# Second norm as a stream of its own and the first FFN unit's sums in PSUM, in a two-path transformer block on one core

## The chip, the cores and the metric

One core of a Trainium2 chip runs the whole program. The metric is the device time of one execution in microseconds (us), the median of several runs. Before the change it is 1468.44 us.

## What is computed

One layer is applied to two groups of rows: 1024 rows of a sample and 128 rows of a prompt, each 1024 wide, all in fp32. A mixer with three head groups (Fourier, mLSTM, S5) is followed by one output projection and a gated residual, then by a modulated norm and a SwiGLU network. Cut to what matters here:

```python
def block(x, mods, p, init, grid):
    sh1, sc1, g1, sh2, sc2, g2 = mods
    xn = rmsnorm(x, p["norm1_w"]) * (1 + sc1) + sh1
    mix, final = mixer(xn, p, init, grid)
    x = x + g1 * mix
    xn = rmsnorm(x, p["norm2_w"]) * (1 + sc2) + sh2
    ff = (jax.nn.silu(xn @ p["w_gate"]) * (xn @ p["w_up"])) @ p["w_down"]
    x = x + g2 * ff
    return x, final
```

The change lies between `x + g1 * mix` and the first of the products with `w_gate` and `w_up`.

## The kernel before, in words

**How the order of the work is made.** The kernel is written as a set of Python generators ("streams"), each with a priority, that yield single instructions. `Weaver.run` (L200) keeps modelled clocks of the engines and at each turn emits the head of the stream that could start first; at equal times the lower priority number goes first. What it emits is the fixed order of each engine's queue, and on the chip each engine takes its queue in that order. A stream waits with `has("name")` for a milestone of another one, `take`/`push`/`used` hand tiles from stream to stream, and `bank` takes one of the eight PSUM banks. An operation given the engine `VP` goes to VectorE or to GpSimd, whichever the model takes to end first. Because every instruction is recorded by one helper, all rows of the profile have the line L146, and tiles' names tell the work apart.

**fp32 products.** `split` (L264) writes a tile as a high part (ScalarE, a cast) and a low part (VectorE, source minus high part). `mm3` makes one product of three matmuls: high × low, low × high, high × high. A product over 512 features is four blocks of 128, that is 12 matmuls of 512 columns.

**The output projection** (`out_project`, L1454) goes in two column halves; in the second, each of the nine row chunks c (0 to 7 the sample, 8 the prompt) has 24 matmuls into one bank. `evac_x1` (L1538) takes a bank: `gt` = bank × gate, `xr` += `gt`, a square with a sum on ScalarE, and `ss`, the sum over both column halves. `xr` are the tiles of x1, five buffers; `x1_feed` (L1529) loads them, and chunks 5 to 8 can only be loaded when earlier buffers come free (`used("x1")`).

**The second norm.** `scaled` (L1549) makes 1/rms of some chunks (`ms`, `y` by pow on GpSimd, `t`, `t`, `t`, `r`) and multiplies the tiles. `affined` (L1554) transposes a 128-column block of four chunks into a bank (four matmuls with `ident`) and writes it through ScalarE with the modulation's scale and shift, to `xt`. `norm_h0` (L1562) does this for chunks 0 to 3, eight blocks k, and splits each block at once into Y11 and Y21 (`y200f`/`y201f` and `y210f`/`y211f` in the profile). `norm_h1` (L1576) starts behind it, with chunks 4 to 7: blocks 0 to 3 give b12, of which Y11's difference T1 is made, blocks 4 to 7 give b22, split into Y22 (`y220f`/`y221f`); then T2, T3 and T4 follow, sums and differences of these blocks for a seven-product scheme. `norm_p` (L1636) does the prompt's chunk 8, eight single transposes (`xtp`, split into `yp00t`/`yp01t`).

**The FFN units.** There are eleven units of 256 hidden columns, each with a gate half and an up half. `weights1` (L1659) splits the raw weights `fraw` into `r10t`/`r11t` (`r0`, upper half of the features), `r20t`/`r21t` (`r1`) and, from unit 1 on, sums `sd` into `sh`/`sl`. The first unit (`first_unit`, L1745) runs plain products: per half and for each of its two 128-column parts d, Y11 with r0, Y21 with r1, T1 with r0 and Y22 with r1; each product has a bank of its own and VectorE adds it in SBUF (`pu`, or `xr` in the up half). T1's result is 12 minus 11, so its sum starts from Y11's. The prompt's products (256 columns) come between. The later units (`gate_or_up`, L1805) run the seven-product scheme. `prompt_store` (L1721) turns the prompt's hidden rows `hp` of the unit before with two transposes and stores them; it is called in `gate_or_up` (L1855) behind the first product of each gate half.

Of the kernel before, what the change touches and what calls it, by code (L numbers as in the profile page):

```python
# [111 lines left out]
class Weaver:  # L112
# [47 lines left out]
    def has(self, *names):  # L160
        return lambda: all(n in self.done for n in names)
# [59 lines left out]
def tile_trunk(ctx, tc, I, O, dbg=None):  # L221
# [61 lines left out]
    def used(name):  # L283
        wv.fed[name][1] += 1
# [1264 lines left out]
    def scaled(cs):  # L1549
        r = yield from rstd_of(ss2[:, cs[0]:cs[-1] + 1], len(cs), D, f"r1{len(cs)}")  # L1550
        for i, c in enumerate(cs):
            yield ts(V, x1[c], x1[c], r[:, i:i + 1], ALU.mult)

    def affined(cs, k, t):  # L1554
        ps, = yield from bank([128, len(cs), 128], keep=1)
        yield [T.transpose(ps[:, i], x1[c][:, k * 128:(k + 1) * 128], ident) for i, c in enumerate(cs)]
        yield has(f"affine1{k // 4}")
        ab, st = AB[2 + k // 4], int(cs[0] == 8)
        yield act(t, ps, AF.Identity, scale=ab[:, k % 4, 0, st:st + 1], bias=ab[:, k % 4, 1, st:st + 1])
        give(ps)  # L1560

    def norm_h0():  # L1562
        yield has(*[f"x1_{c}" for c in range(4)])
        yield from scaled(range(4))
        for k in range(8):
            if k % 4 == 0:
                yield has(f"ob{k // 4}")
                Y["12"[k // 4] + "1"] = [unit("f", k // 4, n, "y2", (4, 512)) for n in range(2)]
            t = xw.tile([128, 512], F32, name="xt", bufs=4)
            yield from affined(range(4), k, t)  # L1570
            hi, lo = Y["12"[k // 4] + "1"]
            yield from split(t, hi[:, k % 4], lo[:, k % 4], V)
        for _ in range(4):
            used("x1")

    def norm_h1():  # L1576
        yield has(*[f"x1_{c}" for c in range(4, 8)], "norm_h0")
        yield from scaled(range(4, 8))
        KS = range(4)
        part = {q: [[u[:, k] for u in Y[q]] for k in KS] for q in ("11", "21")}  # L1580

        def f(q, k):
            return [u.bitcast(F32) for u in part[q][k]]

        def unit_of(i, name):
            yield has(f"wo{i}")
            return wo_unit(i, name).rearrange("p (k t) -> p k t", k=4)

        def new(q, *at):
            us = []  # L1590
            for n, i in enumerate(at):
                us.append((yield from unit_of(i, f"{q}{n}")))
            Y[q] = us
            part[q] = [[u[:, k] for u in us] for k in KS]
        b12 = []
        for k in KS:
            b12.append(xw.tile([128, 512], F32, name="xt", bufs=4))
            yield from affined(range(4, 8), k, b12[k])
            d = xw.tile([128, 512], F32, name="xd", bufs=2)
# [6 lines left out]
        b22 = (yield from unit_of(2, "b22")).bitcast(F32)  # L1606
        for k in KS:
            yield from affined(range(4, 8), k + 4, b22[:, k])
# [4 lines left out]
        for _ in range(4):  # L1613
            used("x1")
        done.update(("22", "x1used"))
# [10 lines left out]
        done.update(("T2", "T3"))  # L1626
        yield from new("T4", 7, 2)
        for k in KS:
            d, e = (xw.tile([128, 512], F32, name=n, bufs=b) for n, b in (("xd", 2), ("xt", 4)))
            yield tt(VP, d, f("21", k)[0], f("T2", k)[0], ALU.subtract)  # L1630
            yield tt(VP, e, f("21", k)[1], f("T2", k)[1], ALU.subtract)
            yield tt(VP, d, d, e, ALU.add)
            yield from split(d, *part["T4"][k], VP)
        done.add("T4")

    def norm_p():  # L1636
# [105 lines left out]
                yield from gate_or_up(i, up, sg, pg)  # L1742


    def first_unit():  # L1745
        gate, val, pg = {}, {}, []
        for up in range(2):
            r0 = yield from take("r0")
            ab = []
            for d in range(2):  # L1750
                ps, = yield from bank([128, 512])
                yield from prod(ps, [t[:, :, d] for t in r0], "11")
                if d == 0:
                    yield has("x1used" if up else "fpu")
                if up:
                    t = xw.tile([128, D], F32, name="xr", bufs=5)
                    ab.append((t[:, 0:512], t[:, 512:1024]))
                else:
                    ab.append([L5["fpu"].tile([128, 512], F32, name="pu", bufs=4) for _ in range(2)])
                yield act(ab[d][1], ps, AF.Copy)  # L1760
                give(ps)

            def finish(q, t):
                if not up:
                    yield act(t, t, AF.Silu)
                    gate[q] = t
                else:
                    yield tt(VP, t, t, gate[q], ALU.mult)
                    val[q] = t

            def rest(r, q, last):
                for d in range(2):
                    ps, = yield from bank([128, 512])
                    yield from prod(ps, [t[:, :, d] for t in r], q)
                    o = ab[d][0 if q == "21" else 1]
                    yield tt(V, o, ab[d][1], ps, ALU.add)
                    give(ps)
                    if last:
                        yield from finish(2 * d + (q != "21"), o)
            r1 = yield from take("r1")  # L1780
            yield from rest(r1, "21", True)
            yield has("T1")
            yield from rest(r0, "T1", False)
            bp, = yield from bank([128, 2, 128], keep=1)
            yield from prompt(bp, 0, r0)
            used("r0")
            yield has("22")
            yield from rest(r1, "22", True)
            yield from prompt(bp, 1, r1)
            used("r1")  # L1790
            hp = yield from prompt_out(0, up, bp, pg, L5["fpu"])
# [12 lines left out]

    def gate_or_up(i, up, sg, pg):  # L1805
# [45 lines left out]
        p1, p5, u2, u3 = (L5["fpu"].tile([128, 512], F32, name="pu", bufs=4) for _ in range(4))  # L1851
        yield act(p1, ba, AF.Copy)
        give(ba)
        if pend:
            yield from prompt_store(*pend.pop())  # L1855
        bp, = yield from bank([128, 2, 128], keep=1)
        yield from prompt(bp, 0, r[0])
        used("r0")
# [11 lines left out]
        yield from spart(ba, "T3")  # L1870
        yield tt(V, u3, u2, ba, ALU.add)
        give(ba)
        yield tt(VP, u2, u2, p5, ALU.add)
        yield tt(VP, p5, u3, p5, ALU.add)
        yield from result(3, p5)
# [69 lines left out]
    ss2 = xw.tile([128, NT], F32, name="ss2")  # L1945
    add("x1evac", evac_x1(), 9)
    add("x1feed", x1_feed(xw), 19)
    add("norm_h0", norm_h0(), 10)
    add("norm_h1", norm_h1(), 11)
    add("norm_p", norm_p(), 12)  # L1950
# [378 lines left out]
```

## Time and profile before

| | us |
|---|---|
| median of 3 runs | 1468.44 (1461.15 to 1475.85) |
| the profiled execution, its own time | 1467.89 |
| its span, first to last instruction | 1466.1 |
| TensorE busy | 1363.1 (93%) |
| weight loads on TensorE | 1120.4 (76%) |
| VectorE busy | 939.4 (64%) |
| ScalarE busy | 533.6 (36%) |
| GpSimd busy | 272.0 (19%) |
| mean granted clock of TensorE | 0.962 of full speed |

How to read it: busy is the time that an engine's instructions run, the span is shared by all, and engines overlap. In the rows below PE is TensorE, DVE VectorE, ACT ScalarE, POOL GpSimd, and SPq the queue that issues the transfers. Matmuls overlap each other, so the pace of TensorE is the distance between starts, not the duration of one. The number in brackets at a row's end is how long the engine had stood before it, and who released it.

### The profile page before, as it was taken

Reading aid. Unit: us, or ns where it says so; the run is one execution under the profiler, and the core shown is the slowest. Engines: PE = TensorE matmul, PEld = TensorE weight load, DVE = VectorE, ACT = ScalarE, POOL = GpSimd, SP = SyncE. Lnnn points to the kernel's source line nnn. Section 1 sums busy time; section 2 is a strip of 40 time slices with the busy share of each in tenths; the row PEclk is TensorE's granted clock in tenths of the full one; section 3 lists DMA queues with packets and bytes.
Section 4 is the critical chain, followed back from the end, with each engine's and each line's share of the span. In section 5 each row is a group of like instructions: output and inputs, shape, how many; then the busy total and the mean of one; then the engine's idle time right before and its main releaser. Section 6 shows DMA issues by size and latency. Waiting matters only on the chain.

```text
span 1466.1 us, 18997 instructions
## 1 busy us (share of the span) xinstructions
PE 1363.1 (93%) x6885; PEld 1120.4 (76%) x6885; DVE 939.4 (64%) x1790; ACT 533.6 (36%) x1059; POOL 272.0 (19%) x350
## 2 busy tenths in 40 slices
PE   7899999988899789797889999999999999999996
PEld 1787788855888678576778888888888877888885
DVE  5956888974144578634685666665676664545897
ACT  3632233433343443314622333333332233443433
POOL 4364455542135011000000000000000010000011
PEclk8999999998999989888999999999999999999999
DMA  9165422154433954133022223312223339735472
GB/s 344 67 180 169 155 90 83 62 195 146 142 107 81 287 165 149 64 143 123 15 70 72 93 91 114 101 69 97 90 98 113 100 120 379 284 110 184 153 247 94
DMA packets 117682, 199.49 MB, mean 136 GB/s; under 512 B 12364, under 2 KB 53684, under 8 KB 117588
## 3 DMA queue, kind: packets, MB, share of 16 engines
q1 hardware_dynamic: 116180, 195.44, 40.2%
q0 software_dynamic: 1408, 2.83, 0.6%
q8 instruction: 54, 0.88, 0.2%
q14 instruction: 40, 0.33, 0.1%
HBM read 151.77 MB, written 46.47 MB: 135 GB/s over the span
## 4 chain that ended last, share of the span: by engine, by line
PE 71%; DVE 14%; DMA 6%; ACT 4%; issue 3%; POOL 1%; SPq 1%; DVEq 0%; POOLq 0%; ACTq 0%
PE bank L146 71%; DMA fraw<-in_w_ada_dram 2%; DMA nb<-nit_d 2%; DVE xo L146 2%; DVE nu L146 1%; SPq L146 1%; DVE xd L146 1%; DVE xr L146 1%; DMA hr<-h_d 1%; ACT L146 1%; DVE T L146 1%; DVE a L146 1%; DMA out_dram<-cn 1%; DVE bp L146 0%; ACT P L146 0%
## 5 line engine op out<-in xcount | busy, mean ns | idle before, releaser
L146 PE MATMUL bank<-ow,oh 128*128 128x512 f32 x912 | 213.6, 394 | 6.8 <-DVE ow L146 6.5
L146 PEld LDWEIGHTS bank<-ow,oh 128*128 128x128 f32 x912 | 173.1, 190 | 44.7 <-DVE ow L146 5.1
L146 PE MATMUL bank<-T,sh 128*128 128x512 f32 x480 | 152.3, 392 | 0.0
L146 POOL TENSOR_TENSOR pu<-pu 128x512 f32<-128x512 f32 x20 | 25.7, 1283 | 475.1 <-DVE pu L146 454.4
L146 DVE TENSOR_TENSOR pu<-pu,bank 128x512 f32<-128x512 f32 x106 | 72.5, 684 | 61.1 <-PE bank L146 59.9
L146 PEld LDWEIGHTS bank<-T,sh 128*128 128x128 f32 x480 | 90.9, 189 | 18.6
L146 PE MATMUL bank<-T,sl 128*128 128x512 f32 x240 | 94.2, 393 | 1.2 <-DVE sl L146 1.2
L146 DVE TENSOR_TENSOR oh<-hr,oh 128x1536 fp32r<-128x1536 f32 (+2 forms) x29 | 45.3, 1561 | 75.9 <-ACT oh L146 75.4
L146 POOL TENSOR_TENSOR y<-ms,nhalf 128x4 f32<-128x4 f32 (+2 forms) x24 | 22.2, 927 | 257.8 <-DVE ms L146 256.8
L146 ACT ACTIVATE oh<-hr 128x1536 fp32r<-128x1536 f32 (+2 forms) x29 | 38.4, 1324 | 84.1 <-PE bank L146 58.3
L146 DVE TENSOR_TENSOR sl<-fraw,sh 128x512 fp32r<-128x512 f32 x40 | 27.7, 692 | 61.2 <-ACT sh L146 60.7
L146 ACT ACTIVATE sh<-sd 128x512 fp32r<-128x512 f32 x40 | 25.3, 633 | 100.8 <-DVE sd L146 55.3
L146 ACT ACTIVATE pu<-bank 128x512 f32<-128x512 f32 x42 | 25.1, 598 | 92.5 <-PE bank L146 90.8
L146 PE MATMUL bank<-fraw,sc 128*32 128x512 f32 x160 | 48.6, 676 | 7.7 <-DMA fraw<-in_w_ada_dram 7.6
L146 PEld LDWEIGHTS bank<-T,sl 128*128 128x128 f32 x240 | 45.4, 189 | 10.3 <-DVE sl L146 1.6
L146 PE MATMUL bank<-T,r20t 128*128 128x512 f32 x160 | 52.8, 391 | 0.0
L146 DVE TENSOR_TENSOR_SCAN xo<-dec,ri 64x296 f32<-64x296 f32 x48 | 45.1, 941 | 1.8 <-POOL ri L146 0.7
L146 PE MATMUL bank<-y201f,r10t 128*128 128x512 f32 x96 | 38.5, 401 | 0.0
L146 PE MATMUL bank<-y200f,r10t 128*128 128x512 f32 x96 | 38.3, 399 | 0.0
L146 PE MATMUL bank<-y200f,r11t 128*128 128x512 f32 x96 | 38.3, 399 | 0.0
L146 ACT ACTIVATE sg<-pu 128x512 f32<-128x512 f32 x40 | 25.0, 624 | 36.0 <-DVE pu L146 36.0
L146 POOL TENSOR_TENSOR acc<-acc,g2bc 128x512 f32<-128x512 f32 x3 | 5.3, 1778 | 175.4 <-DVE acc L146 175.4
(604 smaller groups left out, 3776.2 us busy)
## 6 DMA issues: line engine op xcount, KB each, us to landing
fraw<-in_w_ada_dram SPq DMA_DIRECT2D x40, 512.0 KB
hr<-h_d SPq DMA_DIRECT2D x21, 768.0 KB
wp<-in_w_down_dram SPq DMA_DIRECT2D x15, 768.0 KB
fraw<-in_w_gate_dram SPq DMA_DIRECT2D x22, 512.0 KB
fraw<-in_w_up_dram SPq DMA_DIRECT2D x22, 512.0 KB
h_d<-sg SPq DMA_DIRECT2D x36, 256.0 KB
wraw<-in_w_feat_dram SPq DMA_DIRECT2D x14, 512.0 KB
h_d<-hs SPq DMA_DIRECT2D x27, 256.0 KB
```

The source lines that it names most:

```text
L146: s.call(*s.a, **s.k)
```

## The change

The second norm is taken apart. A stream `norm_scale` scales each half's four chunks as three and one. A stream `norm_turned` does all transposes and evictions, twelve blocks into `xt` (four buffers, handed on by `push`) and the last four into b22, and frees the `xr` buffers; `norm_h0` and `norm_h1` only take blocks and split them. T4's source is built in the block's own buffer while T2 and T3 are made: 21 minus `d`, plus the low part. In the first unit the bank of Y11's product stays open: ScalarE copies it, and Y21's product is added to it in PSUM; in the same way Y22's is added to T1's. SiLU and the product gate × up then read the bank for the first of the two results. `prompt_store` is called later in each gate half, behind the T3 product.

```diff
+    def norm_scale():
+        for h in range(2):
+            for cs in (range(4 * h, 4 * h + 3), [4 * h + 3]):
+                yield has(*[f"x1_{c}" for c in cs])
+                yield from scaled(cs)
+            done.add(f"scaled{h}")
+    def norm_turned():
+        f = wv.fed["nx"]
+        for n in range(12):
+            h, k = divmod(n, 8)
+            yield has(f"scaled{h}")
+            yield lambda n=n: n - f[1] < 4
+            t = xw.tile([128, 512], F32, name="xt", bufs=4)
+            yield from affined(range(4 * h, 4 * h + 4), k, t)
+            push("nx", t)
+            if n == 7:
+                for _ in range(4):
+                    used("x1")
+        L5["b22"] = (yield from unit_of(2, "b22")).bitcast(F32)
+        for k in range(4):
+            yield from affined(range(4, 8), k + 4, L5["b22"][:, k])
+            done.add(f"b22{k}")
+        for _ in range(4):
+            used("x1")
+        done.add("x1used")
     def norm_h0():
-        yield has(*[f"x1_{c}" for c in range(4)])
-        yield from scaled(range(4))
         for k in range(8):
...
-            t = xw.tile([128, 512], F32, name="xt", bufs=4)
-            yield from affined(range(4), k, t)
+            t = yield from take("nx")
             hi, lo = Y["12"[k // 4] + "1"]
             yield from split(t, hi[:, k % 4], lo[:, k % 4], V)
-        for _ in range(4):
-            used("x1")
+            used("nx")
     def norm_h1():
-        yield has(*[f"x1_{c}" for c in range(4, 8)], "norm_h0")
-        yield from scaled(range(4, 8))
+        yield has("norm_h0")
...
-            b12.append(xw.tile([128, 512], F32, name="xt", bufs=4))
-            yield from affined(range(4, 8), k, b12[k])
+            b12.append((yield from take("nx")))
...
             yield from split(d, *part["T2"][k], VP)
             yield from split(b12[k], *part["T3"][k], VP)
+            yield tt(VP, b12[k], f("21", k)[0], d, ALU.subtract)
...
+            yield tt(VP, b12[k], b12[k], f("21", k)[1], ALU.add)
         yield from new("T4", 7, 2)
         for k in KS:
-            d, e = (xw.tile([128, 512], F32, name=n, bufs=b) for n, b in (("xd", 2), ("xt", 4)))
-            yield tt(VP, d, f("21", k)[0], f("T2", k)[0], ALU.subtract)
-            yield tt(VP, e, f("21", k)[1], f("T2", k)[1], ALU.subtract)
-            yield tt(VP, d, d, e, ALU.add)
-            yield from split(d, *part["T4"][k], VP)
+            yield from split(b12[k], *part["T4"][k], VP)
     def first_unit():
...
+            def finish(q, t, src):
+                if not up:
+                    yield act(t, src, AF.Silu)
+                    gate[q] = t
+                else:
+                    yield tt(V if src is not t else VP, t, src, gate[q], ALU.mult)
+                    val[q] = t
+            def upon(ps, w, q, first, last):
+                for k in range(4):
+                    yield mm3(ps, w[0][:, k], w[1][:, k], Y[q][0][:, k], Y[q][1][:, k], first and k == 0, last and k == 3, q == "21")
...
             for d in range(2):
-                ps, = yield from bank([128, 512])
-                yield from prod(ps, [t[:, :, d] for t in r0], "11")
...
+                pa.extend((yield from bank([128, 512])))
+                yield from upon(pa[d], w0[d], "11", True, True)
...
-                yield act(ab[d][1], ps, AF.Copy)
-                give(ps)
+                yield act(ab[d][1], pa[d], AF.Copy)
             r1 = yield from take("r1")
-            yield from rest(r1, "21", True)
+            w1 = [[t[:, :, d] for t in r1] for d in range(2)]
+            for d in range(2):
+                yield from upon(pa[d], w1[d], "21", False, True)
+                yield from finish(2 * d, ab[d][0], pa[d])
+                give(pa[d])
             yield has("T1")
-            yield from rest(r0, "T1", False)
+            pb = []
+            for d in range(2):
+                pb.extend((yield from bank([128, 512])))
+                yield from upon(pb[d], w0[d], "T1", True, False)
             bp, = yield from bank([128, 2, 128], keep=1)
             yield from prompt(bp, 0, r0)
             used("r0")
             yield has("22")
-            yield from rest(r1, "22", True)
+            for d in range(2):
+                yield from upon(pb[d], w1[d], "22", False, True)
+                yield tt(V, ab[d][1], ab[d][1], pb[d], ALU.add)
+                give(pb[d])
+                yield from finish(2 * d + 1, ab[d][1], ab[d][1])
     def gate_or_up(i, up, sg, pg):
...
         yield act(p1, ba, AF.Copy)
         give(ba)
-        if pend:
-            yield from prompt_store(*pend.pop())
...
         yield from spart(ba, "T3")
         yield tt(V, u3, u2, ba, ALU.add)
         give(ba)
+        if pend:
+            yield from prompt_store(*pend.pop())
+    add("norm_scale", norm_scale(), 9.5)
+    add("norm_turned", norm_turned(), 9.8)
```

Three places of the queues show what moves. VectorE, the scaling of chunks 0 to 3 before (`gt` and `xr` are the residual's steps, `ss` the sum of squares):

```order
L146 TENSOR_TENSOR ss_6301<-ssh 128x1
L146 TENSOR_SCALAR ms<-ss_6301 128x4
L146 TENSOR_TENSOR t<-y 128x4
L146 TENSOR_TENSOR t<-t,ms 128x4
L146 TENSOR_SCALAR t<-t 128x4
L146 TENSOR_TENSOR r<-y,t 128x4
L146 TENSOR_SCALAR xr<-xr,r 128x1024 x2
```

and VectorE in the same place now:

```order
L146 TENSOR_SCALAR ms<-ss_6301 128x3
L146 TENSOR_TENSOR t<-y 128x3
L146 TENSOR_TENSOR t<-t,ms 128x3
L146 TENSOR_SCALAR t<-t 128x3
L146 TENSOR_TENSOR r<-y,t 128x3
L146 TENSOR_SCALAR xr<-xr,r 128x1024 x2
L146 TENSOR_TENSOR gt<-bank_6416,g_6302 128x512
L146 TENSOR_SCALAR xr<-xr,r 128x1024
L146 TENSOR_TENSOR xr<-xr,gt 128x512
L146 TENSOR_TENSOR ss_6301<-ssh 128x1
L146 TENSOR_SCALAR ms<-ss_6301 128x1
L146 TENSOR_TENSOR t<-y 128x1
```

Chunks 0 to 2 are scaled ahead of chunk 3's residual, and chunk 3 has a chain of its own behind it.

TensorE behind the out-projection before, the second part d of Y11's product and what follows it (`ident,xr` are transposes of the second norm, four to a block; `y211f,r20t` is Y21's product):

```order
L146 MATMUL bank_6560<-y200f,r10t 128x512
L146 MATMUL bank_6754<-ident,xr 128x128 x4
L146 MATMUL bank_6781<-y201f,r10t 128x512
L146 MATMUL bank_6781<-y200f,r11t 128x512
L146 MATMUL bank_6781<-y200f,r10t 128x512
```

and TensorE from the out-projection's last matmul on now:

```order
L146 MATMUL bank_6701<-wo_6315,mt20t 128x512
L146 MATMUL bank_6617<-y201f,r10t 128x512
L146 MATMUL bank_6617<-y200f,r11t 128x512
L146 MATMUL bank_6617<-y200f,r10t 128x512
L146 MATMUL bank_6760<-ident,xr 128x128 x4
```

Before, the first block of chunks 4 to 7 stood behind twelve matmuls of the first product; now it stands behind three, and the eight blocks are spread over Y11's two products.

TensorE at the end of unit 1's first gate product before (`ident,hp` turn the prompt's hidden rows, `r11t,yp00t` is the prompt's product):

```order
L146 MATMUL bank_7288<-y201f,r10t 128x512
L146 MATMUL bank_7288<-y200f,r11t 128x512
L146 MATMUL bank_7288<-y200f,r10t 128x512
L146 MATMUL bank_7306<-ident,hp_7266 128x128 x2
L146 MATMUL bank_7314<-r11t,yp00t 128x256
```

and TensorE at the end of the T3 product of the same half now:

```order
L146 MATMUL bank_7348<-T_6991,sh 128x512
L146 MATMUL bank_7348<-T_6990,sl 128x512
L146 MATMUL bank_7348<-T_6990,sh 128x512
L146 MATMUL bank_7368<-ident,hp_7257 128x128 x2
L146 MATMUL bank_7381<-y211f,r20t 128x512
L146 MATMUL bank_7381<-y210f,r21t 128x512
```

The two transposes have moved behind the prompt's twelve matmuls and the products T1, T2 and T3, ahead of Y21's product.

## Rows read from the trace of the kernel before

**Rows 1.** The chain that ended last, from 773 us on: start, us, what.
```profile
772.93 429.02 PE bank L146 x2117
```

**Rows 2.** Stretches: length, busy us (instructions) of PE, PEld, DVE, ACT, POOL, then clock, DMA, GB/s.
```profile
680.25:772.93 92.68, 73.61 (x333) 59.51 (x331) 67.32 (x117) 38.83 (x69) 1.55 (x2) 0.87 0.19 69
...
700.00:710.00 10.00, 9.26 (x55) 7.43 (x53) 5.92 (x10) 8.15 (x15) 0.00 (x0) 1.00 0.00 1
...
750.00:760.00 10.00, 6.41 (x34) 5.19 (x32) 10.00 (x17) 3.85 (x6) 0.00 (x0) 1.00 0.00 1
...
780.00:880.00 100.00, 100.00 (x495) 84.83 (x494) 64.72 (x93) 33.13 (x53) 5.14 (x4) 1.00 0.25 83
```

**Rows 3.** Who TensorE waited for, 680 to 773 us: total, times, longest.
```profile
PE bank L146 <- issue: 7.3, 1, 7.3
PE bank L146 <- DVE hp L146: 5.2, 1, 5.2
PE bank L146 <- DVE T L146: 2.4, 2, 2.2
...
PE bank L146 <- DVE sl L146: 1.2, 1, 1.2
PE bank L146 <- DVE xr L146: 1.1, 3, 0.8
```

**Rows 4.** TensorE in order of time: start us, us, engine, line, operation, out<-in.
```profile
654.30 0.39 PE L146 MATMUL bank<-wo,mf10f 128*128 128x512 f32 x1
...
676.37 0.60 PE L146 MATMUL bank<-ident,xr 128*128 128x128 f32 x4
676.73 0.48 PE L146 MATMUL bank<-wo,mf20f 128*128 128x512 f32 x1
...
694.14 0.63 PE L146 MATMUL bank<-y200f,r10t 128*128 128x512 f32 x1
...
698.41 0.63 PE L146 MATMUL bank<-y211f,r20t 128*128 128x512 f32 x1
...
723.81 0.50 PE L146 MATMUL bank<-y221f,r20t 128*128 128x512 f32 x1 [1.28 <-DVE y221f L146]
...
739.73 0.39 PE L146 MATMUL bank<-T,r10t 128*128 128x512 f32 x1
...
745.17 0.28 PE L146 MATMUL bank<-r11t,yp00t 128*128 128x256 f32 x1
...
746.60 0.40 PE L146 MATMUL bank<-y221f,r20t 128*128 128x512 f32 x1
```

**Rows 5.** VectorE in order of time, the residual and the norm's sums.
```profile
645.88 0.16 DVE L146 TENSOR_TENSOR ss<-ssh 128x1 f32<-128x1 f32 x1 [0.85 <-ACT gt L146]
...
649.79 0.69 DVE L146 TENSOR_TENSOR xr<-xr,gt 128x512 f32<-128x512 f32 x1
...
651.33 0.16 DVE L146 TENSOR_TENSOR ss<-ssh 128x1 f32<-128x1 f32 x1 [0.85 <-ACT gt L146]
...
653.60 0.75 DVE L146 TENSOR_SCALAR xr<-xr,r 128x1024 f32<-128x1024 f32 x1
...
679.87 0.69 DVE L146 TENSOR_TENSOR xr<-xr,gt 128x512 f32<-128x512 f32 x1
```

**Rows 6.** GpSimd in order of time, the norm's pow.
```profile
651.77 1.01 POOL L146 TENSOR_TENSOR y<-ms,nhalf 128x4 f32<-128x4 f32 x1 [43.85 <-DVE ms L146]
...
695.90 0.55 POOL L146 TENSOR_TENSOR y<-ms,nhalf 128x1 f32<-128x1 f32 x1 [7.10 <-DVE ms L146]
```

**Rows 7.** The transfers' queue, the first load of chunk 5.
```profile
676.68 0.34 SPq L146 DMA_DIRECT2D xr<-in_x_sample_dram  x1
```

**Rows 8.** The tile pu: its instructions, count, ns least/median/most, first and last start.
```profile
L146 DVE TENSOR_TENSOR pu<-pu,bank x106: 674/686/689, 702.1 to 1204.7; 128x512 f32<-128x512 f32 x106
...
L146 ACT ACTIVATE pu<-pu x4: 633/634/635, 704.3 to 730.2; 128x512 f32<-128x512 f32 x4
```

**Rows 9.** Who VectorE waited for, 775 to 1200 us.
```profile
DVE pu L146 <- POOL pu L146: 29.2, 20, 1.5
```

More of the change, by code (lines that the diff above doesn't have):

```diff
@@ L1560, in affined, with unit_of @@
         give(ps)
+    def unit_of(i, name):
+        yield has(f"wo{i}")
+        return wo_unit(i, name).rearrange("p (k t) -> p k t", k=4)
+    def norm_turned():
[17 more added lines that the diff above has]
+        done.add("x1used")
+    wv.fed["nx"] = [[], 0]
     def norm_h0():
-        yield has(*[f"x1_{c}" for c in range(4)])
-        yield from scaled(range(4))
         for k in range(8):
@@ L1583, in f @@
             return [u.bitcast(F32) for u in part[q][k]]
-        def unit_of(i, name):
-            yield has(f"wo{i}")
-            return wo_unit(i, name).rearrange("p (k t) -> p k t", k=4)
         def new(q, *at):
@@ L1605, in norm_h1 @@
         done.add("T1")
-        b22 = (yield from unit_of(2, "b22")).bitcast(F32)
+        b22 = None
         for k in KS:
-            yield from affined(range(4, 8), k + 4, b22[:, k])
+            yield has(f"b22{k}")
+            b22 = L5["b22"]
             if k == 0:
@@ L1612, in norm_h1 @@
             yield from split(b22[:, k], *[u[:, k] for u in Y["22"]], VP)
-        for _ in range(4):
-            used("x1")
-        done.update(("22", "x1used"))
+        done.add("22")
         for k in KS:
@@ L1625, in norm_h1 @@
             yield from split(b12[k], *part["T3"][k], VP)
-        done.update(("T2", "T3"))
+            yield tt(VP, b12[k], f("21", k)[0], d, ALU.subtract)
+            if k == 3:
+                done.update(("T2", "T3"))
+            yield tt(VP, b12[k], b12[k], f("21", k)[1], ALU.add)
         yield from new("T4", 7, 2)
         for k in KS:
-            d, e = (xw.tile([128, 512], F32, name=n, bufs=b) for n, b in (("xd", 2), ("xt", 4)))
-            yield tt(VP, d, f("21", k)[0], f("T2", k)[0], ALU.subtract)
-            yield tt(VP, e, f("21", k)[1], f("T2", k)[1], ALU.subtract)
-            yield tt(VP, d, d, e, ALU.add)
-            yield from split(d, *part["T4"][k], VP)
+            yield from split(b12[k], *part["T4"][k], VP)
         done.add("T4")
@@ L1747, in first_unit @@
         for up in range(2):
+            def finish(q, t, src):
[8 more added lines that the diff above has]
+                    yield mm3(ps, w[0][:, k], w[1][:, k], Y[q][0][:, k], Y[q][1][:, k], first and k == 0, last and k == 3, q == "21")
             r0 = yield from take("r0")
-            ab = []
+            w0 = [[t[:, :, d] for t in r0] for d in range(2)]
+            pa, ab = [], []
             for d in range(2):
-                ps, = yield from bank([128, 512])
-                yield from prod(ps, [t[:, :, d] for t in r0], "11")
-                if d == 0:
-                    yield has("x1used" if up else "fpu")
+                pa.extend((yield from bank([128, 512])))
+                yield from upon(pa[d], w0[d], "11", True, True)
+            yield has("x1used" if up else "fpu")
+            for d in range(2):
                 if up:
@@ L1759, in first_unit @@
                     ab.append([L5["fpu"].tile([128, 512], F32, name="pu", bufs=4) for _ in range(2)])
-                yield act(ab[d][1], ps, AF.Copy)
-                give(ps)
[L1763 to L1779, printed above, removed]
-            r1 = yield from take("r1")
-            yield from rest(r1, "21", True)
+                yield act(ab[d][1], pa[d], AF.Copy)
+            r1 = yield from take("r1")
+            w1 = [[t[:, :, d] for t in r1] for d in range(2)]
[3 more added lines that the diff above has]
+                give(pa[d])
             yield has("T1")
-            yield from rest(r0, "T1", False)
+            pb = []
+            for d in range(2):
+                pb.extend((yield from bank([128, 512])))
+                yield from upon(pb[d], w0[d], "T1", True, False)
             bp, = yield from bank([128, 2, 128], keep=1)
@@ L1787, in first_unit @@
             yield has("22")
-            yield from rest(r1, "22", True)
+            for d in range(2):
+                yield from upon(pb[d], w1[d], "22", False, True)
+                yield tt(V, ab[d][1], ab[d][1], pb[d], ALU.add)
+                give(pb[d])
+                yield from finish(2 * d + 1, ab[d][1], ab[d][1])
             yield from prompt(bp, 1, r1)
```

## The prediction

> **What bounds the kernel now.** I read three views. First the chain that ended last: from 772.93 us it stays on TensorE for 429 us without a break [rows 1], so time is won only where TensorE waits or runs slowly. Then the stretches [rows 2]: from 780 to 880 us TensorE is busy for the whole 100 us, at a granted clock of 1.00; but from 680.25 to 772.93, which is the second half of norm 2, the first FFN unit and the start of the next, it is busy 73.61 of 92.68 us, at 0.87. This is the stretch that the change rewrites; up to some 645 us the two programs issue the same work in the same order. Last, who it waits for there [rows 3], and how its products follow each other [rows 4].
>
> What should the stretch cost? Counted from the code, it has 228 products of 512 columns, 60 of 256 (the prompt's), 40 transposes of the features and 2 of the prompt's hidden rows. At full clock 24 products take 745.17 − 739.73 = 5.44 us, twelve prompt products 746.60 − 745.17 = 1.43, and a group of four transposes 676.73 − 676.37 = 0.36, with 0.08 more for the product behind it [rows 4]. That makes 51.7 + 7.15 + 4.4 + 0.2 = 63.4 us. **So 92.7 − 63.4 = 29.3 us are lost here**, the most that the change can win in this place. Of these, 18.5 are waits: 7.3 and 1.1 for rows of x1 that are not scaled yet, 2.4 for the parts of T1, 5.2 for the prompt's hidden rows, 1.2 for a split weight [rows 3], 1.28 for block 22 [rows 4]. Most of the rest is the clock: behind the wait of 7.3 us ten products, from 694.14 to 698.41, come 0.427 us apart instead of 0.227, half speed, that is 1.2 instead of 2.4 GHz. Behind the wait of 1.28 us at 723.81 they don't [rows 4].
>
> **The change part by part.** *The stream of transposes.* Now the xr buffers of chunks 0 to 3 come free when the eighth group of transposes is through, at 676.37 [rows 4], because each group waits for the split before it; the loads of chunks 5 to 8 start at 676.68 [rows 7], and the norm's second half is late by that. In the changed order the first group stands ahead of chunk 5's first product, which starts at 654.30 [rows 4], and the eighth 30 products later: 654.3 + 0.4 (a wait, below) + 30 × 0.227 + 8 × 0.44 = 665.0. The loads start 11.7 us earlier. ScalarE's evictions and casts of these groups, 16 at 0.6 us or a little more, end two or three us behind it; each group has a bank of its own, so TensorE isn't held by them.
>
> *The norm in threes and ones.* Three columns come first, then chunk 3 alone. From a sum of squares to the first scaling takes 653.60 − 651.33 = 2.27 us with four columns [rows 5]; with one it is 0.46 less, since pow on GpSimd takes 0.55 instead of 1.01 [rows 6]. Three columns are not in the trace: between these two, and I take 1.01, the nearer in width. Chunk 2's sum is at 645.88, so the first scaling starts at 648.15; two scalings, chunk 3's eviction, a scaling and then chunk 3's addition follow, 0.6 to 0.7 each, so this starts at 650.75 instead of 649.79; its sum 1.54 later [rows 5], its own scaling 1.8 behind that, 0.7 long: ready at 654.8. TensorE comes at 654.3 with three other transposes to do first: 0.4 lost. The scaling has also to wait until the store of the tile to x_d has read it. How long a store takes isn't shown: nothing more, or 0.7 more if it takes what chunk 5's load does from its issue at 676.68 to its use at 679.87 [rows 5, 7]; I take nothing, since the store itself starts at the addition's end, 2.7 us ahead.
> For chunk 7 the same steps are 2.2 + 1.8 + 0.7, and 1.3 for the three other scalings and the step that stand in between: 6 us behind its last product. TensorE meanwhile has chunk 8's 24 products, three more and three transposes, 6.4: 0.1 lost at most. Chunk 8 is evicted only behind that; a weight split and five steps of the queue precede its scaling. VectorE's steps follow each other 0.6 us apart where it is full (17 in 10 us, [rows 2]). So it is ready 9.1 us behind the end of the out-projection, and TensorE, after 24 products and 7 groups, is there at 8.4: 0.7 lost. In place of 7.3 + 1.1 and their slow clock: 1.2 us.
>
> *Sums in PSUM.* Eight additions leave VectorE, and T4 takes two steps per block instead of three, four fewer: 12 steps of 0.6, 7.2 us, gone from the queue that from 750 to 760 has no pause [rows 2] and in which hp, T1's parts and the split weight stand. The SiLU now reads a bank. That isn't in the trace: from SBUF it takes 0.63, and VectorE's addition from a bank 0.69 [rows 8]; I take 0.63, the same engine's, and it ends no wait either way. The product gate × up from a bank is that of the addition, 0.69.
> New waits: product 21 may begin in a bank only when ScalarE has copied 11 out of it. Following ScalarE's new queue, the two copies end near 688.4 and 692.6; TensorE comes at 690.5 (680.25 + 0.4 + 24 products + 8 groups + 0.9 of waits) and 2.7 later. Nothing is lost; without this cover it would be a step of ScalarE, 0.6 each. T1's last part is ready a microsecond before it is needed. Tight is the up half: r1's low part waits on VectorE for a cast that stands on ScalarE behind the second SiLU, and comes 1.1 us after TensorE: 1.1 lost.
>
> *Prompt's features turned later.* TensorE goes from the next unit's product 11 straight to the prompt and T1, whose weights are split 6 us before. hp is wanted 9 us later and is made earlier: its wait of 5.2 goes, and with it the fall of the clock. The third split weight now stands ahead of the addition that it waited behind: 1.2. In the ten gate halves the addition u2 + p5 moves from GpSimd to VectorE. There VectorE waits for GpSimd 29.2 us in 20 cases, 1.46 each [rows 9]; it now spends 0.3 + 0.6 on two steps instead. TensorE waits for neither, so I count nothing; if the cover were gone it would be a few tenths in each half.
>
> **Sum.** 29.3 are lost now; 0.4 + 0.1 + 0.7 + 1.1 = 2.3 remain or are new, each shorter than the 1.28 behind which the clock held. Won: 27.0 us. The profiled execution took 1467.89 (its span of 1466.1 and 1.8 around it), 0.55 under the median of the three runs, 1468.44. 1468.4 − 27.0 = 1441.4, and with half a microsecond for small waits that I don't see, **1442**. The lead isn't given back later: behind it TensorE waits for nothing for 429 us [rows 1], with DMA at a quarter of its share [rows 2].
>
> One rule speaks against this. The row first: from 700 to 710 products and transposes alternate as they will through the whole first gate half now, TensorE was busy 9.26 of them, and the granted clock was 1.00 [rows 2]. The Trainium skill (TensorE: Matmul & The Clock Gate, "A second HAM failure mode: psum-queue depth-cycling") says that frequent short pauses between groups of matmuls, as banks are cycled, make the clock fall and rise again and again, so that throughput drops though a single matmul is as fast as ever. This window of the trace doesn't agree; what the rule would give is rival C.
>
> **The rivals.**
> A is my forecast: chance 0.65, 1442 us, of itself 1437 to 1447.
> B, the waits come back elsewhere. Four chains end within a microsecond or so of TensorE's arrival: chunks 3, 7 and 8, and r1 in the up half. If each is 1.5 us later, that is 6 us, and two of them would pass the length at which the clock falls, at ten products × 0.2 us and a little more, 2.5 each: 11 us given back, 1453. For it: VectorE is busy 73% of the stretch [rows 2], and its queue is in order. Against: each of these waits was longer before. Chance 0.20.
> C, the clock stays low through the mixed first gate half: its first 72 products at 0.427 instead of 0.227 cost 14.4 us, the win is 12.6, and the time 1456. For it the rule, against it the window from 700 to 710. Chance 0.07.
> D, the change wins its place but the lead ends at something else, the loads of the next units' weights: 1466. Against: DMA at 0.25 [rows 2], and these loads wait for buffers that come free earlier too. Chance 0.05.
> E, slower: in each of the ten gate halves TensorE stands at the moved transposes, or at a split weight held up by the two steps that VectorE has there now. At a wait of 2.2 us and 1.6 of slow clock each that is 38 us, less the 27 won: 1479. It decides from 2.7 us per half on. For it: two steps more in that queue; against: 1.46 us of waiting less in the same place, and TensorE without a pause from 780 to 880. Chance 0.03.
>
> **How the numbers follow.** 1% is 14.7 us, about what a measurement of this kernel can tell from no change. Faster by more: A and B, 0.85. Within it: C and D, 0.12. Slower: E, 0.03. The range's low end is all 29.3 us and 4 for the spread of the runs, 1435; its high end takes in B and C, 1456.
>
> **What would show it.** Right: the loads of chunks 5 to 8 near 665; the first unit's products within a microsecond behind the out-projection's last; some 66 us instead of 92.7 from there to the next unit's T3; no wait of TensorE over 1.5 us in it, none for hp, and a granted clock of 0.97 or more. Wrong: a wait of over 2 us at the transposes of chunk 7 or 8 (B), a clock under 0.8 with short waits only (C), TensorE waiting in the units behind (D and E).

## The result, and the profile after

The changed kernel takes **1444.76 us**, the median of 4 runs (1443.11 to 1446.22), beside 1468.61 for the kernel before (1461.15 to 1475.85): an estimated ratio of 0.985, with a 95% interval of 0.9822 to 0.9878. The forecast was 1442, in a range of 1435 to 1456.

The stretches of the changed kernel, in the columns of [rows 2]. The first answers to its 680.25:772.93: from the end of the output projection to the second matmul of the next unit's T3. The last, called **the stretch** from here on, reaches from the end of chunk 4's products to the next unit's product Y21 in its gate half, so that both programs have the same work in it:

```profile
682.99:751.29 68.30, 65.74 (x330) 55.09 (x329) 53.81 (x88) 35.72 (x62) 0.93 (x1) 0.98 0.16 54
682.99:692.18 9.19, 9.19 (x59) 7.83 (x58) 7.63 (x17) 7.84 (x13) 0.93 (x1) 1.00 0.25 86
700.00:710.00 10.00, 10.00 (x53) 8.39 (x52) 8.79 (x16) 6.04 (x13) 0.00 (x0) 1.00 0.01 2
780.00:880.00 100.00, 100.00 (x495) 84.78 (x495) 70.41 (x104) 31.06 (x48) 2.59 (x2) 1.00 0.27 93
...
656.52:753.93 97.41, 94.06 (x472) 78.43 (x470) 71.89 (x124) 50.08 (x88) 2.35 (x3) 0.98 0.25 85
```

The same stretch of the kernel before:

```profile
654.30:775.59 121.29, 102.15 (x471) 82.85 (x470) 79.60 (x135) 52.34 (x89) 1.55 (x2) 0.90 0.20 69
```

So 121.29 - 97.41 = 23.9 us are won here. The whole span is 22.7 shorter (1466.1 to 1443.4): the new profile reaches the stretch 2.2 us later (656.52 for 654.30), the units behind it take 0.55 more (from Y21 to the first matmul of the down projection 429.59, before 429.04), and what follows takes 1.6 less. None of the waits of [rows 3] is left; two others stand in the changed kernel from 642 to 760 us:

```profile
PE bank L146 <- ACT xr L146: 2.6, 1, 2.6
PE bank L146 <- DVE xr L146: 0.8, 1, 0.8
```

The second is for chunk 3, which the prediction put at 0.4 us; the first was not foreseen. TensorE in order of time, as in [rows 4]:

```profile
656.52 0.49 PE L146 MATMUL bank<-ident,xr 128*128 128x128 f32 x3
657.81 0.33 PE L146 MATMUL bank<-ident,xr 128*128 128x128 f32 x1 [0.79 <-DVE xr L146]
...
682.77 0.39 PE L146 MATMUL bank<-wo,mt20t 128*128 128x512 f32 x1
682.99 0.39 PE L146 MATMUL bank<-y201f,r10t 128*128 128x512 f32 x1
...
712.29 0.40 PE L146 MATMUL bank<-y201f,r10t 128*128 128x512 f32 x1
...
717.53 0.39 PE L146 MATMUL bank<-y200f,r10t 128*128 128x512 f32 x1
720.48 0.50 PE L146 MATMUL bank<-y211f,r20t 128*128 128x512 f32 x1 [2.56 <-ACT xr L146]
...
724.46 0.40 PE L146 MATMUL bank<-y210f,r21t 128*128 128x512 f32 x1
...
727.65 0.39 PE L146 MATMUL bank<-T,r10t 128*128 128x512 f32 x1
```

The first unit starts 0.22 us behind the projection's last matmul, with chunks 4 to 7 ready. But at the up half's product Y21 TensorE stands, and the ten matmuls from 720.48 to 724.46 take 3.98 us instead of 2.27. The up half's Y11 and Y21 together, from 712.29 to the start of T1's product at 727.65, take 15.36 us. ScalarE in these us:

```profile
716.18 1.04 ACT L146 ACTIVATE r20t<-fraw 128x1024 fp32r<-128x1024 f32 x1
717.13 0.36 ACT L146 ACTIVATE hp<-bank 128x256 f32<-128x256 f32 x1
719.31 0.63 ACT L146 ACTIVATE T<-xd 128x512 fp32r<-128x512 f32 x1 [1.82 <-DVE xd L146]
719.85 0.58 ACT L146 ACTIVATE xr<-bank 128x512 f32<-128x512 f32 x1
```

and VectorE:

```profile
717.46 1.22 DVE L146 TENSOR_TENSOR r21t<-fraw,r20t 128x1024 fp32r<-128x1024 f32 x1
718.60 0.68 DVE L146 TENSOR_TENSOR xd<-xd,y201f 128x512 f32<-128x512 f32 x1
```

Product Y21 adds to the bank of Y11, which ScalarE must have copied first (`xr<-bank`, 719.85). ScalarE is free for it from 717.49, but ahead of it in ScalarE's queue stands a cast (`T<-xd`) that waits for VectorE, where `xd` stands behind the split of r21t. The split is through at 718.68, the copy only at 720.43.

### The profile page after: what moved, and what is told of

Its sections match the earlier page's. It is cut to its first block, busy times and chain, and to the rows that moved or that the text cites. A ratio compares the mean times of both kernels' runs of the same rounds, so it can differ in the third digit from the quotient of the medians.

```text
span 1443.4 us, 19010 instructions
## 1 busy us (share of the span) xinstructions
PE 1350.3 (94%) x6885; PEld 1113.9 (77%) x6885; DVE 941.0 (65%) x1798; ACT 532.3 (37%) x1059; POOL 260.6 (18%) x342
## 4 chain that ended last, share of the span: by engine, by line
PE 71%; DVE 12%; DMA 7%; ACT 3%; issue 3%; POOL 2%; SPq 1%; DVEq 0%; POOLq 0%; ACTq 0%
PE bank L146 71%; DMA fraw<-in_w_ada_dram 3%; DVE xo L146 2%; DMA nb<-nit_d 2%; SPq L146 1%; DVE nu L146 1%; DMA hr<-h_d 1%; DMA v_d<-vt 1%; DVE a L146 1%; DMA out_dram<-cn 1%; DVE bp L146 0%; DVE t L146 0%; ACT P L146 0%; ACT L146 0%; DVE h L146 0%
## 5 line engine op out<-in xcount | busy, mean ns | idle before, releaser
L146 POOL TENSOR_TENSOR pu<-pu 128x512 f32<-128x512 f32 x10 | 12.9, 1287 | 475.4 <-DVE pu L146 475.4
L146 DVE TENSOR_TENSOR sl<-fraw,sh 128x512 fp32r<-128x512 f32 x40 | 27.7, 693 | 63.4 <-ACT sh L146 62.9
L146 POOL TENSOR_TENSOR y<-ms,nhalf 128x1 f32<-128x1 f32 (+2 forms) x26 | 23.4, 902 | 247.2 <-DVE ms L146 246.3
L146 PE MATMUL bank<-y211f,r20t 128*128 128x512 f32 x96 | 39.4, 410 | 2.6 <-ACT xr L146 2.6
L146 PE MATMUL bank<-y210f,r20t 128*128 128x512 f32 x96 | 38.3, 399 | 0.0
L146 PE MATMUL bank<-y210f,r21t 128*128 128x512 f32 x96 | 38.0, 396 | 0.0
```

The costliest lines, as they stand in the source:

```text
L146: s.call(*s.a, **s.k)
```

## The experiments

Two theories. **Q**: the late second half of the norm was the whole cause; VectorE was late with T1, hp and the split weights only because the norm's steps fell among theirs. **T**: the three parts each win their own waits, as the prediction added them. And for the new wait, **R** (the copy) against **W** (the weight). Medians of runs don't tell variants a few us apart: from one profile to another the stretch begins between 654.2 and 661.6 us, though TensorE's order of the work is the same up to there. So the stretch is read from each trace; the changed kernel, profiled twice, has 97.41 and 97.15. One part of it moves by itself, though: at its start TensorE's wait for chunk 3, behind which VectorE waits for the store to x_d, is anything from nothing to 1.44 us in the runs that scale three and one, whose order up to there is the same. A difference of about a microsecond therefore counts only with that wait taken out.

**The norm alone**, on the kernel before (T4's new form with it):

```diff
+    add("norm_scale", norm_scale(), 9.5)
+    add("norm_turned", norm_turned(), 9.8)
...
-            yield from affined(range(4), k, t)
+            t = yield from take("nx")
```

> The kernel before with the norm's part of the change alone (norm_scale, norm_turned, T4 built in the block's buffer); first unit with sums in SBUF and the prompt's transposes behind the first product, as before. The stretch from the end of chunk 4's products to the next unit's product Y21 took 121.3 us before and 97.4 in the changed kernel. Theory Q (the norm's late second half is the cause, and VectorE is late everywhere behind it only for that): the waits for T1's parts, block 22 and hp go too, the stretch takes 95 to 98 us, the time is that of the changed kernel, 1441 to 1446. Rival T (the three parts each win their own waits, as the prediction added them): the waits for hp (5.2 us and about 2.7 of slow clock) and for T1's parts (2.4 and 2) come back, 103 to 108 us, 1451 to 1456.

Measured: 1446.63 us, ratio 0.9842 (0.981 to 0.9874). The stretch, and TensorE's waits in it:

```profile
658.18:754.62 96.44, 92.77 (x471) 77.31 (x470) 76.38 (x133) 50.69 (x89) 2.34 (x3) 1.00 0.26 87
```
```profile
PE bank L146 <- DVE xr L146: 1.4, 1, 1.4
PE bank L146 <- DVE T L146: 1.3, 1, 1.3
PE bank L146 <- DVE hp L146: 0.9, 1, 0.9
```

The stretch is a microsecond shorter than the whole change makes it, within Q's 95 to 98 and well under T's 103 to 108. VectorE does nearly all its old steps (76.38 us, before 79.60) and is 0.9 us late with hp instead of 5.2; the clock is 1.00 throughout. Q holds in the main and T falls; but the waits for T1's parts (1.3) and hp shrink and don't go, as Q had said, and the median lies just above Q's 1441 to 1446. What in the norm's part does it (the earlier transposes, the buffers that come free earlier, T4's new form) this run doesn't separate.

**The norm undone** in the changed kernel, which leaves the sums in PSUM and the later transposes:

```diff
-    add("norm_scale", norm_scale(), 9.5)
-    add("norm_turned", norm_turned(), 9.8)
...
+        yield has(*[f"x1_{c}" for c in range(4, 8)], "norm_h0")
+        yield from scaled(range(4, 8))
```

> The changed kernel with the norm's part undone: sums in PSUM and the prompt's later transposes stay. Theory Q: the waits for chunks 4 to 7 (7.3 us and 1.1) and the slow clock behind them stay, T1's parts are as late as before; only hp's wait and that for a split weight go: 121.3 - 9 = about 112 us for the stretch, 1458 to 1460. Rival T (each part wins its own): VectorE's eight additions less bring T1's parts and block 22 in time as well, 105 to 108, 1452.

Measured: 1465.35 us, ratio 0.997 (0.9952 to 0.9988).

```profile
658.77:772.85 114.08, 100.24 (x471) 81.21 (x470) 75.06 (x126) 51.88 (x88) 1.55 (x2) 0.93 0.22 74
```

Two parts of three win 7.2 us of the stretch's 23.9; Q said about 112, T 105 to 108.

**The prompt's transposes alone**, and **the sums in PSUM alone**, on the kernel before:

```diff
         give(ba)
-        if pend:
-            yield from prompt_store(*pend.pop())
         bp, = yield from bank([128, 2, 128], keep=1)
...
         yield tt(V, u3, u2, ba, ALU.add)
         give(ba)
+        if pend:
+            yield from prompt_store(*pend.pop())
```

> The kernel before with only the prompt's transposes moved behind the T3 product. Theory Q (the wait moves on): hp is no longer waited for, but VectorE is still full, TensorE comes to T3 at about 763 and its split weight, now behind hp, the last differences of the first unit and the sum of T2, is ready only at about 767: a wait of 4 to 5 us there and slow clock behind it, the stretch 116 to 119 us instead of 121.3, 1462 to 1466. Rival T (the move wins what the prediction gave it, 5.2 + 2.7 + 1.2): 112 us, 1457 to 1459.

```diff
-                yield from prod(ps, [t[:, :, d] for t in r0], "11")
+                yield from upon(pa[d], w0[d], "11", True, True)
...
-                    yield tt(V, o, ab[d][1], ps, ALU.add)
+                yield from upon(pa[d], w1[d], "21", False, True)
```

> The kernel before with only the first unit's sums in PSUM. Theory Q (the late norm stays): the wait of 7.3 us for chunks 4 to 7 stays, a wait of 2 us for ScalarE's copy comes in, T1's parts are late as before; VectorE has eight additions less, so hp comes some 5 us earlier and its wait of 5.2 falls under 2: 121.3 - 5 = 114 to 118 us for the stretch, 1460 to 1466. Rival T (as the prediction added the parts): hp, the split weight and T1's parts are all in time, 107 to 111, 1454 to 1458.

Measured: 1465.91 us (ratio 0.9988, 0.9966 to 1.0009) and 1465.43 (0.997, 0.9951 to 0.9989). Of the prompt's run the stretch and the longest waits:

```profile
657.03:773.29 116.26, 99.10 (x471) 80.31 (x470) 79.45 (x134) 51.96 (x88) 1.55 (x2) 0.94 0.22 73
```
```profile
PE bank L146 <- issue: 7.3, 1, 7.3
PE bank L146 <- ACT sh L146: 4.0, 1, 4.0
```

and of the sums' run:

```profile
655.38:772.38 117.00, 101.11 (x471) 82.17 (x470) 75.29 (x127) 52.28 (x89) 1.55 (x2) 0.91 0.21 71
```
```profile
PE bank L146 <- issue: 4.6, 1, 4.6
PE bank L146 <- DVE hp L146: 3.5, 1, 3.5
```

The prompt's move does what Q said of it: hp's 5.2 become 4.0 at T3's weight, and 5.0 us are won. The sums win 4.3; hp still comes 3.5 late, more than the 2 expected.

**The prompt's move undone**, and **the sums in PSUM undone**, in the changed kernel; the diffs are the two above, turned round.

> The changed kernel with the prompt's transposes put back behind the first product of each gate half. Theory M (the move itself removed the wait of 5.2 us for hp and the slow clock behind it, as the prediction had it): the wait comes back, 5 us and 2 to 3 of slow clock, 1452. Theory Q (VectorE's shorter queue removed it): in the changed kernel hp starts on VectorE at 742.20 and is done at 742.62, TensorE's first product of that half ends at 744.17, so the transposes would not wait for it even in the old place: the time is that of the changed kernel within 1 us, and the move is worth nothing here.

> The changed kernel with the first unit's old form: every product in a bank of its own, VectorE adds in SBUF, eight additions of 0.69 us more on VectorE. Theory S (as the prediction had it: VectorE's queue needs the relief): T1's parts, the split weights or hp come late again, one or two waits of 2 to 5 us, the time 1448 to 1455. Rival P (the sums in PSUM bring a wait of their own, 2.56 us and 2.0 of slow clock, and relieve an engine that was no longer late): with the old form product Y21 has a bank of its own, that wait shrinks to the 0.9 for the weight or goes, and the time is 1440 to 1445, as fast as the changed kernel or faster.

Measured: 1444.95 us (ratio 0.9843, 0.9817 to 0.9869) and 1444.37 (0.9841, 0.9814 to 0.9867). The stretch without the prompt's move:

```profile
654.24:750.42 96.18, 92.54 (x472) 77.35 (x470) 71.89 (x125) 50.31 (x89) 2.34 (x3) 1.00 0.26 88
```

and without the sums in PSUM:

```profile
658.77:754.14 95.37, 92.77 (x472) 77.22 (x470) 75.89 (x132) 50.23 (x88) 2.34 (x3) 1.00 0.26 86
```

M and S fall, Q and P stand: on top of the norm neither part wins anything as built. Without the prompt's move the stretch is 1.2 us shorter: hp is ready in time, and the clock didn't fall behind the copy's wait of 2.55 us, which alone is worth 1.7 (more below). Without the sums it is 2.0 shorter: each product has a bank of its own again and waits for no copy, which is worth more than the 1.30 us for which TensorE now waits for T1's parts.

**The copy**: in the up half it is written right behind each product. **The copy and the weight**: besides, the gate half's last SiLU is written behind the up half's `take("r1")`.

```diff
                 yield from upon(pa[d], w0[d], "11", True, True)
-            yield has("x1used" if up else "fpu")
-            for d in range(2):
                 if up:
+                    yield has("x1used")
...
+                    yield act(ab[d][1], pa[d], AF.Copy)
```

> Only the up half of the first unit differs from the changed kernel: ScalarE's copy of each Y11 product out of its bank is written right behind that product, so in ScalarE's queue the first copy stands ahead of a cast for T4 instead of behind it. Theory R (the copy is the wait): the changed kernel's longest wait of TensorE, 2.56 us at 720.48, is for this copy, which stood behind a cast that waited 1.82 us for VectorE. With the copy ahead, only the weight r21t holds TensorE (its split ends at 718.68, TensorE comes at 717.76): a wait of about 0.9 us, no slow clock behind it (ten matmuls 0.43 apart become 0.23, 2.0 us). Time 2.56 - 0.9 + 2.0 = 3.7 us less: about 1441 where the changed kernel takes 1444.8. Rival W (the weight is the wait, as the prediction had it): the wait stays at 2 us or more, the clock falls as before, and the time is the same within 1 us.

```diff
             r1 = yield from take("r1")
+            if late:
+                yield act(late[0], late.pop(), AF.Silu)
```

> As the run with the early copy, and the gate half's last SiLU is written behind the up half's taking of the weight r20t/r21t, so that the weight's cast goes ahead of it on ScalarE. Theory R: the cast then starts at about 713.8 instead of 716.18, as soon as TensorE has read the gate half's weight (712.3), its split on VectorE ends near 717, TensorE doesn't wait at Y21 at all: 0.9 us less than with the early copy alone, 4.6 less than the changed kernel, about 1440. Rival: the SiLU that is late now holds up the casts for T4 or the last product of the up half, a new wait of 1 us or more appears behind 720, and the time is that of the early copy or more.

Measured: 1444.4 us (ratio 0.984, 0.9812 to 0.9869) and 1443.2 (0.9837, 0.981 to 0.9864). The stretches, the copy's first:

```profile
659.95:753.71 93.76, 92.78 (x472) 77.27 (x470) 71.58 (x124) 50.04 (x88) 2.34 (x3) 1.00 0.26 88
```
```profile
657.92:750.81 92.89, 92.66 (x471) 77.20 (x470) 71.30 (x124) 50.05 (x88) 2.34 (x3) 1.00 0.27 89
```

97.41 - 93.76 = 3.65 us and 97.41 - 92.89 = 4.5. W falls: with the copy ahead, TensorE waits 0.2 us for r21t. That the two gains are so near R's 3.7 and 4.6 is partly luck. R expected 0.9 us of waiting for the weight, and in the second run the wait for chunk 3 happens to be gone. The up half itself, from Y11 to T1, comes down from 15.36 us to 11.81 and 11.55 (715.62 to 727.43, and 712.98 to 724.53): the copy's edit is worth 3.55 us there and the weight's 0.26 more, not 0.9. With the copy in time the sums in PSUM are worth 95.37 - 93.76 = 1.6 us, 0.5 of it the wait for chunk 3 (1.19 beside 0.68). The medians don't show these gains: both intervals hold the changed kernel's 0.985, and R's 1441 and 1440 didn't come.

**T4 undone**, built as before, in the changed kernel:

```diff
-            yield tt(VP, b12[k], f("21", k)[0], d, ALU.subtract)
...
+            yield tt(VP, d, f("21", k)[0], f("T2", k)[0], ALU.subtract)
+            yield tt(VP, e, f("21", k)[1], f("T2", k)[1], ALU.subtract)
+            yield tt(VP, d, d, e, ALU.add)
```

> The changed kernel with T4 built as before, three steps per block behind T2 and T3 instead of two among them: four steps of 0.6 to 0.7 us more on VectorE. Theory L (T4 has time to spare, and it was the cast for T4's neighbours in ScalarE's queue that held the copy): no new wait; the copies now stand behind a cast that doesn't wait as long, TensorE's wait at Y21 falls from 2.56 to 1 to 2 us, the stretch 94 to 96.5. Theory V (VectorE's queue is still what counts, as the prediction's twelve steps had it): the split weights or hp of unit 1 come late by 2 us or more, 98 to 101, 1446 to 1449.

Measured: 1443.71 us, ratio 0.982 (0.9787 to 0.9853).

```profile
654.78:748.43 93.65, 92.72 (x471) 77.28 (x470) 73.28 (x128) 50.24 (x88) 2.34 (x3) 1.00 0.26 88
```
```profile
PE bank L146 <- DVE sl L146: 0.7, 1, 0.7
PE bank L146 <- ACT sh L146: 0.3, 1, 0.3
```

```profile
709.69 0.40 PE L146 MATMUL bank<-y201f,r10t 128*128 128x512 f32 x1
...
720.61 0.39 PE L146 MATMUL bank<-T,r10t 128*128 128x512 f32 x1
```

With more steps on VectorE the stretch is 3.8 us shorter: ScalarE's order is another one, the copies start at 714.35 and 715.35 behind casts that don't wait, and the up half from Y11 to T1 takes 10.92 us instead of 15.36. This is 4.4 us; 0.9 more comes from chunk 3, for which TensorE doesn't wait here. But L's "no new wait" is wrong: the next unit's split weights come 0.28 and 0.66 us late, and from its T1 to its Y21 it takes 9.86 us (738.57 to 748.43) instead of 8.33. V's 98 to 101 didn't come.

**Four chunks scaled at once**; **the best** adds the copy's and the weight's edits to it; and **the changed kernel again**, with no edit.

```diff
-            for cs in (range(4 * h, 4 * h + 3), [4 * h + 3]):
+            for cs in (range(4 * h, 4 * h + 4),):
```

> The changed kernel with each half's four chunks scaled at once instead of three and one. The scheduler then puts the first transposes twelve products later (2.7 us), so they don't wait for chunk 3 (0.8 us in the changed kernel), and the loads of chunks 5 to 8 start 2.7 us later. Theory N: these loads have time to spare by now, TensorE waits nowhere for it, the stretch is shorter by the wait, 96 to 97.5 us, and three and one is worth nothing. Rival O (order matters, as the prediction had it, each us of the norm counts): chunk 7 comes 2 to 3 us late for its transposes and the clock falls behind the wait, 100 us or more, 1447 to 1449.

> The changed kernel with both edits at the up half (the copy behind each product, the last SiLU behind the weight's cast) and each half's four chunks scaled at once. Theory R: the two waits that the changed kernel has left, 0.8 us for chunk 3 and 2.56 for the copy, are both gone, the stretch takes 92 to 92.7 us (copy_and_weight took 92.9 with the scaling in three and one), 1439 to 1442 beside 1444.8. Rival: scaled at once, chunk 7 and the weight are late by 0.2 to 3 us as in the run with the four at once, where the copy's wait grew to 3.1: the stretch 93 to 96, no gain over copy_and_weight.

> The changed kernel once more, unaltered, for a second profile. In its first profile TensorE waited 2.56 us for the copy and ten matmuls behind it ran at half speed; with the prompt undone the wait was 2.55 us and none did. Theory C (whether the clock falls behind a wait of this length differs from one execution to the next): the wait is again 2.5 us and the clock may stay up; the stretch is then 95.4 instead of 97.4. Rival D (the order of the instructions decides it): the wait, the fall of the clock and the stretch of 97.4 come again.

Measured: 1448.95 us (ratio 0.9864, 0.9839 to 0.989), 1446.26 (0.983, 0.98 to 0.986) and 1446.39 (0.9835, 0.9805 to 0.9866). The stretch with four at once, and of the best:

```profile
661.56:759.38 97.82, 94.48 (x472) 78.29 (x470) 72.34 (x122) 49.89 (x88) 1.55 (x2) 0.98 0.25 84
```
```profile
658.14:752.18 94.04, 93.22 (x471) 77.13 (x470) 72.22 (x122) 49.83 (x88) 1.55 (x2) 1.00 0.27 88
```

Scaled at once, the stretch is 0.4 us longer, just above N's 96 to 97.5 and far from O's 100: chunk 3's wait goes and the copy's grows to 3.1. As built, three and one is worth no more than that. The "best" isn't: 94.04 beside 92.89. Up to the first unit both take the same (25.74 and 25.76 us), so with the copy in time three and one is worth 1.2 us behind that point; what makes it so is not shown. Again, the changed kernel waits 2.55 us for the copy, and the clock falls again, as that run's D said.

## Why the prediction was right, and where it wasn't

**The bound and the price of the stretch** hold: 63.4 us of work were counted, 68.30 are taken, and 4.4 of the 4.9 between them are the up half's, below. The loads of chunk 5 start 11.3 us behind the stretch's start; 10.7 were worked out, 22.4 it was before:

```profile
667.86 0.33 SPq L146 DMA_DIRECT2D xr<-in_x_sample_dram  x1
```

**Chunk 3**: forecast 0.4 us, measured 0.79. Sum to scaling and the rest came as worked out (pow of three columns 0.85); the wait for the store to x_d, taken as nothing, was 0.91, and from nothing to 1.54 in the other runs that scale three and one:

```profile
657.00 0.75 DVE L146 TENSOR_SCALAR xr<-xr,r 128x1024 f32<-128x1024 f32 x1 [0.91 <-DMA x_d<-xr]
```

**Chunks 7 and 8**: forecast 0.1 and 0.7, measured nothing.

**The up half**: this step failed. The prediction followed ScalarE's queue for the two copies of the gate half alone, wrote "nothing is lost", and gave the up half 1.1 us for r1's low part. The copy there took 2.72 of TensorE's time (717.53 to 720.48, less one step) and the clock 1.71 more: 4.4 for 1.1. The run with T4 undone, where TensorE waits for neither copy nor weight, takes 4.4 less there; the run with the copy early takes 3.55 less and still waits for the weight. By the terms, 27.0 - 0.4 + 0.8 - 3.3 = 24.1 against 23.9 measured: this is the shortfall.

**The parts' shares** were wrong, though the sum was nearly right. The prediction took hp's wait from the move of the transposes, and T1's and hp's lateness partly from fewer steps on VectorE. The norm alone gives 24.9 us, the other two 5.0 and 4.3 alone, and as built nothing on top of it. The sum could come out because all three parts are in the change, so that each wait had to go whichever part took it; the time was right for a reason that is partly not the one given. The move on GpSimd costs nothing, as counted: VectorE's waits for it, [rows 9], halve; here from 775 to 1180 us:

```profile
DVE pu L146 <- POOL pu L146: 14.6, 10, 1.5
```

**The rivals.** B came in one of its four places, the up half, by another cause. C didn't come: the clock is 1.00 from 682.99 to 692.18, where products and transposes alternate. The rule of the Trainium skill (TensorE: Matmul & The Clock Gate, "A second HAM failure mode: psum-queue depth-cycling") doesn't show in this profile, nor in the stretch of any other run here: wherever the norm's transposes alternate with products and TensorE doesn't stop, the clock is 1.00. D and E didn't come. As in [rows 1], the chain stays on TensorE from the last wait of the stretch to the end of the units, which cost 0.55 us more in all:

```profile
720.48 460.36 PE bank L146 x2264
```

## What to carry to other kernels

Several waits behind one late stage are not several prizes: advance the stage first, and measure what is left for the other edits. A product that adds to a bank that another engine still has to read waits for that engine's queue, so follow that queue at every place where the form occurs; the scheduler here counts when data is ready and when a buffer comes free, not this wait. Where runs scatter by more than an edit is worth, compare the same work between the same two instructions of two traces, and look which part of it moves without any edit.

## What was not expected

The same wait doesn't always bring the clock down. Before, TensorE waited 2.17 us for T1's parts at 713.01 and the granted clock fell (0.54 in the mean of 712.5 to 715 us, where 0.50 is the lower level, 1.2 GHz); in the run with the prompt alone it waited 2.16 us in the same place, at 715.25, in the same order of instructions, and it stayed at 1.00. Behind the copy it fell after 2.56 and 2.55 us in the changed kernel and not after 2.55 in the run with the prompt's move undone, though the order up to there is the same. The changed kernel, profiled twice, fell twice, so no run shows a difference within one kernel. In the stretches of all these profiles no wait up to 1.44 us that began at full clock was followed by a fall, and every one from 3.09 us on was. The Trainium skill (TensorE: Matmul & The Clock Gate, "What's actually happening") says that the chip watches the activity freely and doesn't start anew with a kernel, so that the moment of a change differs from run to run; that would allow such differences, but no run here tests it. What decides between these stays open; a price of 1.7 us for it was part of the up half's 4.4.
